# Fetching the tokens of two expert units at once, from two rounded parts of the normalised input

## The chip, the cores and the metric

The kernel runs on one core of one Trainium2 chip. The metric is the time of one execution on the device in microseconds; a kernel's time is the median of its runs. Engines are named as in the profile: PE is TensorE (matmuls), PEld its weight loads, DVE VectorE, ACT ScalarE, POOL GpSimd, and SP the engine whose queue issues the transfers that matter here.

## What is computed

The reference is a network of two blocks with two layers each, on 256 tokens of width 1024, all in fp32. The part that counts is the mixture of experts at the end of each layer of the second block:

```
x = _layernorm(alpha * x + mix, ln1_g[l], ln1_b[l])
ffn = _hier_moe(x, ...)            # 4 groups x 8 experts, top group, then top 2 in it
x = _layernorm(alpha * x + ffn, ln2_g[l], ln2_b[l])

def expert_block(args):
    xe, e = args                   # tokens sent to expert e
    hid = jax.nn.silu(xe @ w_gate[e]) * (xe @ w_up[e])
    return hid @ w_down[e]         # FFN width 256
```

Each expert's weights are 1024x512 (gate and up) and 256x1024 (down): 3 MiB, 96 MiB for the 32 experts of a layer. The first block has the same structure with RMS norm and an FFN width of 512; its experts use the same function with `centred` false.

## The kernel before

`moe` computes one layer of experts. The 32 experts are cut into 11 units; in block 2 their form is `wwwnwnwnnnw`. A w unit has 2 experts with room for 64 tokens each, an n unit 4 experts with room for 32 each, so every unit fills 128 rows. The first three units have fixed experts (0 to 5); the other places are given to the experts by how many tokens they have, by `Ranks`: its last product (L737) and a cast (L739) give the sorted numbers kidx, which SP loads into registers (L766) to address the weights of units 3 to 10.

A unit goes through these steps. `select` (L865) builds P, a 128-token by 128-row matrix per token half: a row's entry is the token's scale r (`tok`, from the norm) where the place number `pos` meets, else 0. `fetch(k)` (L871 and L879, for unit 0 `fetch_all`, L871, L877 and L879) multiplies eight 128x128 pieces of x by P in fp32 and applies scale and shift, which gives xg, the tokens of the unit, transposed. L1003 multiplies them by the gate and up weights (tile A), L1006 and L1007 form hid, `second` (L920) multiplies by the down weights (tile B), splits the result into two rounded parts yh and yl (L922, L923), and `combine` (L933) adds them back to the tokens in PSUM. `back` (L942 to L950) makes the weighted transposed P for that. While the products of unit n run, the select and fetch steps of unit n+1 are placed between them: half of them before the second product of the previous unit is complete, half behind it.

The weights pass through a ring of 1 MiB slots: 13 of the base and `EXTRA` more (9 in both blocks). The transfers are issued by SP at L176, in the order A0 A1 B0 A2 B1, then those that need kidx: A3 B2 A4 B3 ... B10, and behind them the weights of the next mixer. A slot can be refilled when the last product that reads it has run. Ahead of the unit before the last (`turn`) stands an `If` (L780) for the case of experts with more than 64 tokens (`overfull`); the branch isn't taken with these inputs, but all engines pass it.

`Head.finish` ends the layer norm ahead of the experts. Per token half it takes mean and variance, r by Ln and Exp (L608, L612), the logits (L621), subtracts the mean from x in place (L619) and a second Exp makes 1/r in `tok`. The residual of the layer multiplies x by r times alpha (L1932 and `residual_2`), and the routing weights are multiplied by 1/r (rwp, L906), because P holds r.

A type F32R (fp32r in the profile) appears in the mixers' products: x and weights are each split into a rounded high part and a low part (L397, L398), and products of the parts are summed.

Of the kernel before, what the change touches and what calls it, by code (L numbers as in the profile page):

```python
# [51 lines left out]
class Core:  # L52
# [25 lines left out]
    def constants(self, ctx):  # L78
# [30 lines left out]
        self.L = cp.tile([128, 2, 36], F32, name="logits")  # L109
        self.tok = cp.tile([128, 2, 4], F32, name="tok")  # L110
        self.gain = cp.tile([128, 8], F32, name="gain")
# [428 lines left out]
class Head:  # L540
# [58 lines left out]
    def finish(self, t):  # L599
        c, nc, p = self.c, self.c.nc, self.p  # L600
        r = c.tok[:, t, 0:1]
        l = p.tile([128, 2], F32, name=f"hl{t}")
        base = self.base[:, 0:36]
        if self.centred:
            mv = p.tile([128, 2], F32, name=f"hmv{t}")
            nc.vector.bn_aggr(mv, self.st[:, t])
            nc.vector.tensor_scalar(c.tok[:, t, 1:2], mv[:, 0:1], -1.0, None, op0=ALU.mult)
            nc.scalar.activation(l[:, 0:1], mv[:, 1:2], AF.Ln, bias=c.col(self.eps))  # L608
        else:
            nc.vector.tensor_scalar(l[:, 1:2], self.st[:, t, 0:1], 1.0 / D, self.eps, op0=ALU.mult, op1=ALU.add)  # L610
            nc.scalar.activation(l[:, 0:1], self.st[:, t, 1:2], AF.Ln, scale=1.0 / D, bias=l[:, 1:2])
        nc.scalar.activation(r, l[:, 0:1], AF.Exp, scale=-0.5)  # L612
        if self.centred:
            nm = p.tile([128, 1], F32, name=f"hnm{t}")
            nc.vector.tensor_scalar(nm, mv[:, 0:1], r, -1.0, op0=ALU.mult, op1=ALU.mult)
            base = p.tile([128, 36], F32, name=f"hb{t}")
            nc.vector.scalar_tensor_tensor(base, self.base[:, 36:72], nm, self.base[:, 0:36], op0=ALU.mult, op1=ALU.add)

            nc.scalar.activation(c.x[:, t], c.x[:, t], AF.Identity, bias=c.tok[:, t, 1:2])  # L619
        nc.scalar.activation(c.tok[:, t, 2:3], l[:, 0:1], AF.Exp, scale=0.5)  # L620
        nc.vector.scalar_tensor_tensor(c.L[:, t], self.q[:, 64 * t:64 * t + 36], r, base, op0=ALU.mult, op1=ALU.add)  # L621
        c.routed = self.end
# [202 lines left out]
def moe(c, ctx, index, scale, shift, w13, w2, nf, spare, centred, residual, end):  # L825
# [22 lines left out]
    extra = c.more(ctx, EXTRA[centred], "ring2", *XO[index])  # L848
    c.warm(sp.tile([128, 512], F32, name="s1")[:, :128], 9, c.routed)
    pos, as_, rest, chosen, counted = router(c, p, mp, c.L)  # L850
    c.warm(sp.tile([128, 512], F32, name="s2")[:, :128], 4, counted)
    places = {"pos": pos}

    def group(unit, first):

        e0, n, cap = unit
        P = p.tile([128, 2, 128], F32, name="P", bufs=2)
        P4 = P.rearrange("p t (g s) -> p t g s", s=cap)
        xg = p.tile([128, 8, 128], F32, name="xg", tag="xg", bufs=2)

        def select():
            at = pos if e0 < fixed else places["pos"]
            for t in range(2):
                for i in range(n):
                    selected = nc.vector.tensor_scalar(P4[:, t, i], c.iota[:, :cap], at[:, t, e0 + i:e0 + i + 1],  # L865
                                                       c.tok[:, t, 0:1], op0=ALU.is_equal, op1=ALU.mult)
            return selected

        def products(q, k, start):
            for t in range(2):  # L870
                nc.tensor.matmul(q, x[:, t, k * 128:(k + 1) * 128], P[:, t], start=start and t == 0, stop=t == 1,  # L871
                                 skip_group_check=True)

        def modulate(q, k, vector):
            o = xg[:, k]
            if vector:
# [4 lines left out]
        def fetch(k):  # L881
            def f():
                q = mp.tile([128, 512], F32, name="ms")[:, :128]
                products(q, k, True)
# [11 lines left out]
    P, xg, steps = group(units[0], True)  # L896
# [41 lines left out]
    def back(pr):  # L938

        e0, ne, cap = pr["unit"]  # L940
        Pw = p.tile([128, 2, 128], F32, name="Pw", bufs=2)
        nc.vector.tensor_mul(Pw.rearrange("p t (g s) -> p t g s", s=cap), P,  # L942
                             (wp if e0 < fixed else wk)[:, :, e0:e0 + ne, None].to_broadcast([128, 2, ne, cap]))
# [21 lines left out]
    for n, unit in enumerate(units):  # L965
        if n:
            P, xg = nxt[:2]
        nxt = group(units[n + 1], False) if n + 1 < len(units) else (None, None, [])
        e0, ne, cap = unit
        last = n == len(units) - 1  # L970
        todo = nxt[2]
        pr = {"n": n, "unit": unit, "h": []}
# [7 lines left out]
        if n == turn:  # L980
# [4 lines left out]
                                   skip_runtime_bounds_check_because="counts of tokens")  # L985
            overfull(c, sp, c.tok, scale, shift, out, w, pos, count, nf, *spare, gate, room,
                     hT, ranks)
# [7 lines left out]
        for u in range(steps_of):  # L995
            ws = begun if begun is not None and u == 0 else first(who, u)
            q = sp.tile([128, 512], F32, name="s1")
            for k in range(8):
                for i in range(128 // cap):

                    m, o = (i, 0) if centred else (i // 2, i % 2)
                    e = u * per + m
                    nc.tensor.matmul(q[cap * i:cap * i + cap, :], xg[:, k, e * cap:(e + 1) * cap],  # L1003
# [899 lines left out]

def residual_2(c, lnp, l, which, out, scale=None):

# [3 lines left out]
    for t in range(2):  # L1909
        nc.vector.scalar_tensor_tensor(out[:, t], c.x[:, t], ALPHA if scale is None else scale[:, t:t + 1], lnp[0],  # L1910
                                       op0=ALU.mult, op1=ALU.mult)
        nc.vector.scalar_tensor_tensor(out[:, t], lnp[1], ALPHA, out[:, t], op0=ALU.mult, op1=ALU.add)


def experts_2(c, l):

    nc, x = c.nc, c.x
    with ExitStack() as ctx:
# [10 lines left out]
        def residual(mp, keep, room, held):  # L1929
            out = keep.rearrange("p (t d) -> p t d", t=2)  # L1930
            sc = c.tok[:, :, 3]
            nc.vector.tensor_scalar(sc, c.tok[:, :, 0], ALPHA, None, op0=ALU.mult)  # L1932
            residual_2(c, [room[:, 0:1024], room[:, 1024:2048]], l, 0, out, sc)
            return out, None
# [324 lines left out]
```

## Time and profile before

| | |
|---|---|
| median of 3 runs | 2397.3 us (2396.76 to 2400.31) |
| the profiled execution | 2401.7 us, of which the span is 2399.7 |
| mean granted TensorE clock | 0.972 of full speed |
| TensorE (PE) busy | 2182.2 us, 91% of the span |
| VectorE (DVE), ScalarE (ACT) busy | 899.4 us, 774.6 us |
| moved by DMA | 775.20 MB, mean 323 GB/s |

The experts of block 2 lie at about 1640 to 1881 us (layer 0) and 2150 to 2386 us (layer 1) of the span. All times of rows are microseconds from the span's start. A window's row gives the busy time of each engine with the count of its instructions, then the granted clock, the DMA share and the rate. In rows of one group of instructions the first numbers are busy time and mean nanoseconds of one, then the idle time before them and what ended it.

### The profile page before, as it was taken

Reading aid. Unit: us, or ns where it says so; the run is one execution under the profiler, and the core shown is the slowest. Engines: PE = TensorE matmul, PEld = TensorE weight load, DVE = VectorE, ACT = ScalarE, POOL = GpSimd, SP = SyncE. Lnnn points to the kernel's source line nnn. Section 1 sums busy time; section 2 is a strip of 40 time slices with the busy share of each in tenths; the row PEclk is TensorE's granted clock in tenths of the full one; section 3 lists DMA queues with packets and bytes.
Section 4 is the critical chain, followed back from the end, with each engine's and each line's share of the span. In section 5 each row is a group of like instructions: output and inputs, shape, how many; then the busy total and the mean of one; then the engine's idle time right before and its main releaser. Section 6 shows DMA issues by size and latency. Waiting matters only on the chain. (4 is left out here: it accounts for less than half of the span.)

```text
span 2399.7 us, 33892 instructions
## 1 busy us (share of the span) xinstructions
PE 2182.2 (91%) x13034; PEld 1268.5 (53%) x13034; DVE 899.4 (37%) x2095; ACT 774.6 (32%) x1561; POOL 44.7 (2%) x48
## 2 busy tenths in 40 slices
PE   7999899988778989998877899999999899999997
PEld 4667633323225865333222387995444678984443
DVE  3864511111003753111100264984222547961232
ACT  3642311111113452211111254562222435642222
POOL 0001000000000200000000000000000000000000
PEclk8999999999999999999999998999999989999999
DMA  9977489999999347999999971556999923559997
GB/s 392 412 266 318 176 369 421 421 422 421 382 422 419 121 184 286 421 421 421 421 420 384 421 284 55 177 193 240 407 417 371 398 88 128 194 176 371 417 387 280
DMA packets 119852, 775.20 MB, mean 323 GB/s; under 512 B 14186, under 2 KB 15594, under 8 KB 35451
## 3 DMA queue, kind: packets, MB, share of 16 engines
q1 hardware_dynamic: 119674, 772.85, 80.1%
q8 instruction: 109, 1.79, 0.3%
q14 instruction: 69, 0.56, 0.1%
HBM read 771.75 MB, written 1.05 MB: 322 GB/s over the span
## 5 line engine op out<-in xcount | busy, mean ns | idle before, releaser
L1003 PE MATMUL s<-w,xg 128*32 128x512 f32 (+1 forms) x3072 | 577.2, 610 | 43.8 <-DMA w<-A 40.9
L920 PE MATMUL s<-w,ht 128*32 128x512 f32 (+1 forms) x1536 | 340.1, 612 | 37.9 <-DMA w<-B 36.4
L1003 PEld LDWEIGHTS s<-w,xg 128*32 128x32 f32 (+1 forms) x3072 | 131.6, 120 | 307.3 <-issue 199.0
L402 PE MATMUL pj<-hi,wh 128*128 128x256 f32 x864 | 242.8, 284 | 3.4 <-ACT sg L1785 2.3
L403 PE MATMUL pj<-lo,wh 128*128 128x256 f32 x864 | 243.2, 283 | 0.0
L871 PEld LDWEIGHTS ms<-P,x 128*128 128x128 f32 x1280 | 170.0, 195 | 138.5 <-ACT xg L879 75.0
L404 PE MATMUL pj<-hi,wl 128*128 128x256 f32 x864 | 240.1, 283 | 0.0
L923 DVE SCALAR_TENSOR_TENSOR yl<-s,ws,yh 128x512 fp32r<-128x512 f32 x88 | 66.1, 751 | 383.5 <-ACT yh L922 383.5
L871 PE MATMUL ms<-P,x 128*128 128x128 f32 x1280 | 208.2, 294 | 1.2
L920 PEld LDWEIGHTS s<-w,ht 128*32 128x32 f32 (+1 forms) x1536 | 80.1, 121 | 224.3 <-issue 147.3
L397 ACT ACTIVATE wh<-w 128x512 fp32r<-128x512 f32 x248 | 154.3, 630 | 119.4 <-PE pj L403 88.3
L398 DVE TENSOR_TENSOR wl<-w,wh 128x512 fp32r<-128x512 f32 x248 | 167.0, 688 | 49.4 <-ACT wh L397 45.1
L402 PEld LDWEIGHTS pj<-hi,wh 128*128 128x128 f32 x864 | 165.7, 192 | 9.1 <-ACT sg L1785 2.8
L404 PEld LDWEIGHTS pj<-hi,wl 128*128 128x128 f32 x864 | 164.0, 192 | 4.9 <-issue 2.4
L403 PEld LDWEIGHTS pj<-lo,wh 128*128 128x128 f32 x864 | 165.8, 192 | 0.5 <-issue 0.3
L865 DVE TENSOR_SCALAR P<-iota,kpos,tok 128x32 f32<-128x32 f32 (+1 forms) x216 | 49.4, 300 | 305.0 <-PE ms L871 304.9
L922 ACT ACTIVATE yh<-s,ws 128x512 fp32r<-128x512 f32 x88 | 60.5, 687 | 315.6 <-PE s L920 280.2
L1007 DVE TENSOR_TENSOR hid<-hid,s 128x256 f32<-128x256 f32 x66 | 27.7, 419 | 338.2 <-ACT hid L1006 338.1
L1006 ACT ACTIVATE hid<-s 128x256 f32<-128x256 f32 x66 | 25.3, 383 | 383.5 <-PE s L1003 383.2
L365 DVE TENSOR_TENSOR wl<-w,wh 128x512 fp32r<-128x512 f32 (+2 forms) x164 | 111.3, 689 | 100.6 <-ACT wh L364 86.0
L364 ACT ACTIVATE wh<-w 128x512 fp32r<-128x512 f32 (+2 forms) x164 | 99.5, 615 | 115.0 <-PE pj L350 55.9
L879 ACT ACTIVATE xg<-ms,mod,gain 128x128 f32<-128x128 f32 x160 | 72.8, 457 | 148.9 <-PE ms L871 146.0
(624 smaller groups left out, 2719.8 us busy)
## 6 DMA issues: line engine op xcount, KB each, us to landing
w<-A SPq DMA_DIRECT2D x384, 1024.0 KB, 19.1
w<-B SPq DMA_DIRECT2D x128, 1024.0 KB, 19.7
w<-B SPq DMA_DIRECT2D x128, 512.0 KB, 11.9
w<-ada SPq DMA_DIRECT2D x48, 1024.0 KB, 10.7
w<-wi SPq DMA_DIRECT2D x48, 1024.0 KB, 8.0
w<-w SPq DMA_DIRECT2D x26, 1024.0 KB, 16.7
w<-wo SPq DMA_DIRECT2D x16, 1024.0 KB, 7.3
w<-wbr SPq DMA_DIRECT2D x8, 1024.0 KB, 4.8
```

What stands on the lines that cost most here:

```text
L364: nc.scalar.activation(wh[:, :n], w[:, k], AF.Copy)
L365: nc.vector.tensor_sub(wl[:, :n], w[:, k], wh[:, :n].bitcast(F32))
L397: nc.scalar.activation(wh, w[:, k], AF.Copy)
L398: nc.vector.tensor_sub(wl, w[:, k], wh.bitcast(F32))
L402: nc.tensor.matmul(d, wh[:, e], hi, start=k == 0 and ch % 2 == 0, stop=False, skip_group_check=True)
L403: nc.tensor.matmul(d, wh[:, e], lo, start=False, stop=False, skip_group_check=True)
L404: nc.tensor.matmul(d, wl[:, e], hi, start=False, stop=k == nk - 1, skip_group_check=True)
L871: nc.tensor.matmul(q, x[:, t, k * 128:(k + 1) * 128], P[:, t], start=start and t == 0, stop=t == 1, skip_group_check=True)
L879: nc.scalar.activation(o, q, AF.Identity, bias=shift[:, k:k + 1], scale=scale[:, k:k + 1])
L920: nc.tensor.matmul(q[cap * i:cap * i + cap, :], ht[:, o * cap:o * cap + cap], pr["w2"][i][:, half, f * 512:f * 512 + 512], start=f == 0, s ...
L923: nc.vector.scalar_tensor_tensor(pr["yl"][:, half], q, pr["ws"], pr["yh"][:, half].bitcast(F32), op0=ALU.mult, op1=ALU.subtract)
L1003: nc.tensor.matmul(q[cap * i:cap * i + cap, :], xg[:, k, e * cap:(e + 1) * cap], ws[m][:, k, 512 * o:512 * o + 512], start=k == 0, stop=k ...
```

## The change

In block 2 the tokens are normalised before they are fetched: `Head.finish` scales x by r and adds -mean times r in one operation, so P holds only zeros and ones, the second Exp, the tok entry for the mean, the multiplication of the routing weights by 1/r and the scale of the residual go. x is kept in two fp32r parts: xh, a rounded copy (ScalarE), and xl = x - xh (`lower`, VectorE, four operations of 128x512). Units 1 to 10 are fetched in pairs, [1,2] to [9,10]: one P and one xg of twice the width for a pair, and per k and token half one product of xh and one of xl with 256 columns, in place of one fp32 product with 128 columns per unit. The eight steps of a pair are spread over its two units. `fetch_all` of unit 0 does all products with xh first, then those with xl. Select makes the ones of all experts of a unit and token half with one comparison of two broadcast tensors. `lower` is placed right behind the first select, ahead of fetch and `Ranks` in the text. The wider P and xg, xh and xl take 24 KB more of each partition: `EXTRA` becomes 9 and 6, so the ring of block 2 has 19 slots and not 22. Block 1 computes as before.

```diff
@@ Head.finish
-            nc.vector.tensor_scalar(c.tok[:, t, 1:2], mv[:, 0:1], -1.0, None, op0=ALU.mult)
...
-            nc.scalar.activation(c.x[:, t], c.x[:, t], AF.Identity, bias=c.tok[:, t, 1:2])
-        nc.scalar.activation(c.tok[:, t, 2:3], l[:, 0:1], AF.Exp, scale=0.5)
+            nc.scalar.activation(c.x[:, t], c.x[:, t], AF.Identity, scale=r, bias=nm)
+        else:
+            nc.scalar.activation(c.tok[:, t, 2:3], l[:, 0:1], AF.Exp, scale=0.5)
@@ moe
+    groups = [[0]] + [[n, n + 1] for n in range(1, len(units), 2)] if centred else [[n] for n in range(len(units))]
+    most = 128 * max(map(len, groups))
+    src = (x,)
+    if centred:
+        src = [p.tile([128, 2, 1024], F32R, name=n) for n in ("xh", "xl")]
+        for t in range(2):
+            nc.scalar.activation(src[0][:, t], x[:, t], AF.Copy)
     pos, as_, rest, chosen, counted = router(c, p, mp, c.L)
...
+    def lower(t):
+        for i in range(2):
+            d = slice(i * 512, i * 512 + 512)
+            nc.vector.tensor_sub(src[1][:, t, d], x[:, t, d], src[0][:, t, d].bitcast(F32))
...
+    def group(ns, first):
+
+        m = 128 * len(ns)
+        P = p.tile([128, 2, most], F32R if centred else F32, name="P", bufs=2)
+        P4 = [P[:, :, 128 * i:128 * i + 128].rearrange("p t (g s) -> p t g s", s=units[n][2]) for i, n in enumerate(ns)]
+        xg = p.tile([128, 8, most], F32, name="xg", tag="xg", bufs=2)
         def select():
-            at = pos if e0 < fixed else places["pos"]
+            for d, (e0, n, cap) in zip(P4, [units[n] for n in ns]):
+                at = pos if e0 < fixed else places["pos"]
+                for t in range(2):
+                    if centred:
+                        selected = nc.vector.tensor_tensor(d[:, t], c.iota[:, None, :cap].to_broadcast([128, n, cap]),
+                                                           at[:, t, e0:e0 + n, None].to_broadcast([128, n, cap]),
+                                                           ALU.is_equal)
...
+        def products(q, k, i, start):
             for t in range(2):
-                nc.tensor.matmul(q, x[:, t, k * 128:(k + 1) * 128], P[:, t], start=start and t == 0, stop=t == 1,
-                                 skip_group_check=True)
+                nc.tensor.matmul(q, src[i][:, t, k * 128:(k + 1) * 128], P[:, t, :m], start=start and t == 0,
+                                 stop=t == 1 and i == len(src) - 1, skip_group_check=True)
...
         def fetch_all():
             qs = [yp.tile([128, 512], F32, name="y", tag="y", bufs=4) for _ in range(4)]
-            for k in range(8):
-                q = qs[k % 4][:, (k // 4) * 128:(k // 4 + 1) * 128]
-                products(q, k, k < 4)
-                modulate(q, k, k % 2)
+            for i in range(len(src)):
+                for k in range(8):
+                    q = qs[k % 4][:, (k // 4) * m:(k // 4 + 1) * m]
+                    products(q, k, i, i == 0 and k < 4)
+                    if i == len(src) - 1:
+                        modulate(q, k, k % 2)
...
     selected = steps[0]()
+    if centred:
+        lower(0)
+        with tc.issue_after(selected.ins):
+            lower(1)
     for f in steps[1:]:
         f()
     with tc.issue_after(selected.ins):
         ranks = Ranks(c, p, mp, as_, fixed, wide, at)
         places["pos"] = ranks.ordered(pos, "kpos")
         w, cnt = rest(ranks.excess)
...
-    wp = p.tile([128, 2, 32], F32, name="rwp")
-    nc.vector.tensor_mul(wp, w, c.tok[:, :, 2:3].to_broadcast([128, 2, 32]))
+    wp = w
...
     for n, unit in enumerate(units):
-        if n:
-            P, xg = nxt[:2]
-        nxt = group(units[n + 1], False) if n + 1 < len(units) else (None, None, [])
+        g = next(i for i, ns in enumerate(groups) if n in ns)
+        at_unit = groups[g].index(n)
+        if at_unit == 0:
+            if n:
+                P, xg = nxt[:2]
+            nxt = group(groups[g + 1], False) if g + 1 < len(groups) else (None, None, [])
+            share = -(-len(nxt[2]) // len(groups[g]))
...
-        todo = nxt[2]
+        todo = [nxt[2].pop(0) for _ in range(min(share, len(nxt[2])))]
...
-EXTRA = (9, 9)
+EXTRA = (9, 6)
```

## Rows read from the trace of the kernel before

**Rows 1.** The page, parts 1 and 2: engines' busy time; rate in 40 slices.

```profile
PE 2182.2 (91%) x13034; PEld 1268.5 (53%) x13034; DVE 899.4 (37%) x2095; ACT 774.6 (32%) x1561; POOL 44.7 (2%) x48
...
GB/s 392 412 266 318 176 369 421 421 422 421 382 422 419 121 184 286 421 421 421 421 420 384 421 284 55 177 193 240 407 417 371 398 88 128 194 176 371 417 387 280
```

**Rows 2.** Windows: length, busy PE, PEld, DVE, ACT, POOL, clock, DMA share, GB/s.

```profile
1660.00:1820.00 160.00, 158.57 (x900) 68.09 (x899) 39.74 (x109) 44.67 (x95) 0.00 (x0) 0.99 1.01 414
1820.00:1840.00 20.00, 18.08 (x129) 8.70 (x128) 2.59 (x5) 5.11 (x11) 0.00 (x0) 1.00 0.75 283
...
2020.00:2060.00 40.00, 40.00 (x352) 40.00 (x351) 38.88 (x78) 22.33 (x41) 0.00 (x0) 1.00 0.59 206
2180.00:2320.00 140.00, 139.25 (x800) 60.25 (x802) 37.73 (x101) 41.21 (x86) 0.00 (x0) 1.00 1.02 416
2320.00:2340.00 20.00, 16.57 (x110) 7.90 (x106) 3.01 (x6) 5.52 (x12) 0.00 (x0) 0.98 0.79 324
2340.00:2360.00 20.00, 19.99 (x138) 9.01 (x130) 2.68 (x5) 5.50 (x12) 0.00 (x0) 0.94 0.98 364
```

**Rows 3.** Issues of tile w on SP, 1650 to 1900, and their landing.

```profile
L176 SPq DMA_DIRECT2D w<-B x56: 328/333/500, 1662.2 to 1862.6; - x56
...
L176 SPq DMA_DIRECT2D w<-A x52: 332/333/1101, 1656.6 to 1842.6; - x52
...
L176 SPq DMA_DIRECT2D w<-lnp x2: 338/338/339, 1765.3 to 1767.7; - x2
...
DMA to landing us min/median/max: 5.5/13.8/20.3
```

**Rows 4.** DMA view, the last B of layer 0: count, KB, us to landing.

```profile
w<-B SPq DMA_DIRECT2D x1, 512.0 KB, 10.2
```

**Rows 5.** Timeline of SP: first and last issues of layer 1's stream.

```profile
2164.53 1.19 SPq L176 DMA_DIRECT2D w<-A  x2
...
2366.70 4.06 SPq L176 DMA_DIRECT2D w<-B  x4
```

**Rows 6.** Waits of SP, 1655 to 1885: total us, times, longest.

```profile
SPq L176 <- PE s L1003: 25.6, 9, 10.6
SPq L766 <- DVE kidx L739: 19.5, 1, 19.5
SPq L780 <- SPq L780: 19.0, 1, 19.0
```

**Rows 7.** Timeline of DVE around the routing of layer 0: start, length.

```profile
1642.40 0.23 DVE L660 SCALAR_TENSOR_TENSOR rpos<-ms,ras 128x64 f32<-128x64 f32 x1 [0.72 <-PE ms L658]
1642.67 0.98 DVE L865 TENSOR_SCALAR P<-iota,rpos,tok 128x64 f32<-128x64 f32 x4
...
1648.99 0.22 DVE L735 TENSOR_SCALAR kperm<-krow,krank 32x32 f32<-32x32 f32 x1
...
1649.38 0.76 DVE L942 TENSOR_TENSOR Pw<-P,rwp 128x256 f32<-128x256 f32 x2
...
1655.72 0.18 DVE L739 CAST kidx<-ms 1x32 int32<-1x32 f32 x1 [1.88 <-PE ms L737]
```

**Rows 8.** Timeline of PE around the routing of layer 0.

```profile
1643.98 3.09 PE L871 MATMUL y<-P,x 128*128 128x128 f32 x16
...
1655.47 0.21 PE L737 MATMUL ms<-kperm,places 32*1 32x32 f32 x2
```

**Rows 9.** Timeline of PE, the last product of either layer.

```profile
1874.22 3.65 PE L920 MATMUL s<-w,ht 128*64 128x512 f32 x16
...
2379.83 3.65 PE L920 MATMUL s<-w,ht 128*64 128x512 f32 x16
```

**Rows 10.** Groups by line and shape, 1660 to 1820: the fetch products.

```profile
L871 PE MATMUL ms<-P,x 128*128 128x128 f32 x256 | 42.4, 292 | 0.2
```

**Rows 11.** The page, part 5: a subtraction into an fp32r low part.

```profile
L398 DVE TENSOR_TENSOR wl<-w,wh 128x512 fp32r<-128x512 f32 x248 | 167.0, 688 | 49.4 <-ACT wh L397 45.1
```

**Rows 12.** Timeline of ACT ahead of the routing of layer 0.

```profile
1636.91 1.14 ACT L619 ACTIVATE x<-x,tok 128x1024 f32<-128x1024 f32 x1
```

More of the change, by code (lines that the diff above doesn't have):

```diff
@@ L109, in constants @@
         self.L = cp.tile([128, 2, 36], F32, name="logits")
-        self.tok = cp.tile([128, 2, 4], F32, name="tok")
+        self.tok = cp.tile([128, 2, 3], F32, name="tok")
         self.gain = cp.tile([128, 8], F32, name="gain")
@@ L852, in moe @@
     places = {"pos": pos}
[L854 to L859, printed above, removed]
-        def select():
-            at = pos if e0 < fixed else places["pos"]
-            for t in range(2):
[L864 to L870, printed above, removed]
-                nc.tensor.matmul(q, x[:, t, k * 128:(k + 1) * 128], P[:, t], start=start and t == 0, stop=t == 1,
-                                 skip_group_check=True)
+    def lower(t):
+        for i in range(2):
+            d = slice(i * 512, i * 512 + 512)
+            nc.vector.tensor_sub(src[1][:, t, d], x[:, t, d], src[0][:, t, d].bitcast(F32))
@@ new lines, in group @@
+    def group(ns, first):
[3 more added lines that the diff above has]
+        xg = p.tile([128, 8, most], F32, name="xg", tag="xg", bufs=2)
+        def select():
+            for d, (e0, n, cap) in zip(P4, [units[n] for n in ns]):
[5 more added lines that the diff above has]
+                                                           ALU.is_equal)
+                        continue
+                    for i in range(n):
+                        selected = nc.vector.tensor_scalar(d[:, t, i], c.iota[:, :cap], at[:, t, e0 + i:e0 + i + 1],
+                                                           c.tok[:, t, 0:1], op0=ALU.is_equal, op1=ALU.mult)
+            return selected
+        def products(q, k, i, start):
+            for t in range(2):
+                nc.tensor.matmul(q, src[i][:, t, k * 128:(k + 1) * 128], P[:, t, :m], start=start and t == 0,
+                                 stop=t == 1 and i == len(src) - 1, skip_group_check=True)
@@ L874, in modulate @@
         def modulate(q, k, vector):
-            o = xg[:, k]
+            o = xg[:, k, :m]
             if vector:
@@ L882, in f @@
             def f():
-                q = mp.tile([128, 512], F32, name="ms")[:, :128]
-                products(q, k, True)
+                q = mp.tile([128, 512], F32, name="ms")[:, :m]
+                for i in range(len(src)):
+                    products(q, k, i, i == 0)
                 modulate(q, k, False)
@@ L889, in fetch_all @@
             qs = [yp.tile([128, 512], F32, name="y", tag="y", bufs=4) for _ in range(4)]
-            for k in range(8):
-                q = qs[k % 4][:, (k // 4) * 128:(k // 4 + 1) * 128]
-                products(q, k, k < 4)
-                modulate(q, k, k % 2)
+            for i in range(len(src)):
+                for k in range(8):
[3 more added lines that the diff above has]
+                        modulate(q, k, k % 2)
         return P4, xg, [select] + ([fetch_all] if first else [fetch(k) for k in range(8)])
-    P, xg, steps = group(units[0], True)
+    P, xg, steps = group(groups[0], True)
     selected = steps[0]()
+    if centred:
+        lower(0)
+        with tc.issue_after(selected.ins):
+            lower(1)
     for f in steps[1:]:
@@ L903, in moe @@
         w, cnt = rest(ranks.excess)
-    wp = p.tile([128, 2, 32], F32, name="rwp")
-    nc.vector.tensor_mul(wp, w, c.tok[:, :, 2:3].to_broadcast([128, 2, 32]))
+    wp = w
+    if not centred:
+        wp = p.tile([128, 2, 32], F32, name="rwp")
+        nc.vector.tensor_mul(wp, w, c.tok[:, :, 2:3].to_broadcast([128, 2, 32]))
     wk = ranks.ordered(wp, "kw")
@@ L941, in back @@
         Pw = p.tile([128, 2, 128], F32, name="Pw", bufs=2)
-        nc.vector.tensor_mul(Pw.rearrange("p t (g s) -> p t g s", s=cap), P,
+        nc.vector.tensor_mul(Pw.rearrange("p t (g s) -> p t g s", s=cap), P[at_unit].bitcast(F32),
                              (wp if e0 < fixed else wk)[:, :, e0:e0 + ne, None].to_broadcast([128, 2, ne, cap]))
@@ L985, in moe @@
                                    skip_runtime_bounds_check_because="counts of tokens")
-            overfull(c, sp, c.tok, scale, shift, out, w, pos, count, nf, *spare, gate, room,
+            overfull(c, sp, None if centred else c.tok, scale, shift, out, w, pos, count, nf, *spare, gate, room,
                      hT, ranks)
@@ L1001, in moe @@
                     m, o = (i, 0) if centred else (i // 2, i % 2)
-                    e = u * per + m
+                    e = at_unit * 128 // cap + u * per + m
                     nc.tensor.matmul(q[cap * i:cap * i + cap, :], xg[:, k, e * cap:(e + 1) * cap],
@@ L1901, in experts_1, with residual_2 @@
             lambda e: expert(c.a["B1"][l], e), 512, (w1_of, w2_of), False, residual, end)
-def residual_2(c, lnp, l, which, out, scale=None):
+def residual_2(c, lnp, l, which, out):
     nc = c.nc
@@ L1909, in residual_2 @@
     for t in range(2):
-        nc.vector.scalar_tensor_tensor(out[:, t], c.x[:, t], ALPHA if scale is None else scale[:, t:t + 1], lnp[0],
-                                       op0=ALU.mult, op1=ALU.mult)
+        nc.vector.scalar_tensor_tensor(out[:, t], c.x[:, t], ALPHA, lnp[0], op0=ALU.mult, op1=ALU.mult)
         nc.vector.scalar_tensor_tensor(out[:, t], lnp[1], ALPHA, out[:, t], op0=ALU.mult, op1=ALU.add)
@@ L1930, in residual @@
             out = keep.rearrange("p (t d) -> p t d", t=2)
-            sc = c.tok[:, :, 3]
-            nc.vector.tensor_scalar(sc, c.tok[:, :, 0], ALPHA, None, op0=ALU.mult)
-            residual_2(c, [room[:, 0:1024], room[:, 1024:2048]], l, 0, out, sc)
+            residual_2(c, [room[:, 0:1024], room[:, 1024:2048]], l, 0, out)
             return out, None
```

## The prediction

> **What bounds the kernel now.** I read the page first. TensorE is busy for 91% of the span and the input stream tops out at 421 to 422 GB/s [rows 1]; both look full, so averages do not say which one sets the two stages that the change touches. The windows do. In 160 us of the first expert stage of block 2 TensorE is busy for 158.57 us and the DMA share is 1.01 at 414 GB/s, and the second layer's stage reads the same [rows 2]. The two are tied, and the question is which one would still take as long if the other became faster.
>
> The ring's queue answers that. After the sorted expert numbers are known it issues 52 transfers of 1 MiB (w<-A), 56 of half a MiB (w<-B) and two lnp rows of half a MiB [rows 3]: 81 MiB. At 421.6 GB/s one MiB takes 2.487 us, so the stream can't be shorter than 201.5 us. It takes, in layer 0, from the first issue at 1656.6 to the last at 1862.6 [rows 3] plus 10.2 us to land [rows 4]: 216.2 us. Layer 1: 2164.53 to the end of the last group of issues at 2370.76, less the issue's own 0.33 [rows 3, 5], plus about the same 10.2: 216.1 us. So 14.7 us per layer are not transfer. Of these about 3.0 are the first landing (5.5 us, the shortest in [rows 3], less 2.5). About 6.6 lie in 1820 to 1840, where the queue delivers 283 of 421 GB/s [rows 2]: the waits show SP at L780 (the `If` of the overfull path) for 19.0 us [rows 6]. What ends that wait is the landing of SP's own transfers, not TensorE. The rest, about 5 us, is spread out.
>
> The start of the stream hangs on routing: SP waits 19.5 us for kidx [rows 6]. The places rpos stand at 1642.40 and kidx is cast at 1655.72, right behind a TensorE product (L737) at 1655.47 [rows 7, 8] that stands in order behind fetch and first expert products. The end of the stage is the last B: in layer 0 it lands at 1872.8, and the sixteen matmuls that need it run 1874.22 to 1877.87 [rows 9], 5.1 us after the landing. In layer 1 they end at 2383.48, 3.0 us after a landing at about 2380.5.
>
> **The change part by part.**
>
> *Fetch, steps of two units.* Now 256 records of L871 take 42.4 us in 160 us, 0.166 each [rows 10]; 8 steps of 4 make 5.3 us a unit and 10.6 a pair. Afterwards a pair takes 8 steps of 4 fp32r matmuls of 256 columns. The mixer window has 352 matmuls in 40.00 us, nearly all of that shape [rows 2], so 0.114 each: 3.6 us a pair. Saved: 7.0 us a pair, five pairs, 35 us of TensorE a layer. What this is worth on the path is another question: the stream needs its 201.5 us whoever computes. I take nothing for it in the middle of the stage. The ACT modulation becomes half as many operations of twice the width, off the path.
>
> *Tail.* With TensorE ahead, the last product should follow the landing in layer 0 as it does in layer 1: 5.1 becomes 2.8, so -2.3; layer 1, 0. Bounds -2.8 and 0.
>
> *Start of the stream.* The 32 fp32 records of unit 0's fetch become 16 with xh and 16 with xl, in fp32r, at 128 columns. The trace has no such product: from 0.057 (half of 0.114) to 0.166 (no gain), 1.8 to 5.3 us for 32. Four subtractions for xl are new, on VectorE; the nearest row is 128x512 at 0.688 [rows 11], so 2.75 us. Two stand ahead of the routing's own operations if the order keeps the text's order, two may fall among them. Against this, L737 now waits 1655.47 - 1643.98 = 11.5 us behind the start of the fetch [rows 8], of which 5.3 are fetch records and the rest are expert products already in hand. If routing is issued by its dependences alone: kperm now stands 6.8 us behind rpos, 3.1 of them behind sixteen fetch records [rows 7, 8]; with about 1.5 of fp32r in their place, 2.75 of subtractions and 0.6 for L737 and the cast that is 8.5 us behind rpos, where kidx now starts 13.3 behind it: -5. If all subtractions and all xl products go first, and unit 0's expert products with them: +1.5 to +3. I take -2 a layer, -4 in all, as 2 to 3 us of fetch records vanish and nothing else in the chain needs xl.
>
> *Head and select.* One small VectorE operation, one Exp and the residual's scale leave the routing chain, some 0.1 to 0.5 us. Scaling x now waits for r; L619 (1.14 us [rows 12]) moves behind Exp, and two copies to xh of the same shape follow: 3 x 1.14 from about 1638.1 is 1641.5, ahead of the select at 1642.67 [rows 7]. Without that cover a copy costs 1.14 us. Select becomes four operations for a pair; 128x256 took 0.38 [rows 7], so at most 1.5 us beside 2 x 0.98 now: VectorE is idle then, nothing on the path. The multiply rwp (0.2 us) goes, off the path.
>
> *The ring, 22 slots to 19.* Three slots are 7.5 us of stream. The queue already waits for TensorE to free slots, 25.6 us in 9 waits, longest 10.6 [rows 6], and no transfer rate is lost by it [rows 2], as the median transfer lands 13.8 us after its issue [rows 3]: about 11 us of earlier ones are still queued. With 19 slots the longest wait would be 10.6 + 7.5 = 18.1, less what TensorE has saved by then (3.5 us a unit; two to three units: 7 to 10). That leaves 8 to 11, about what is absorbed now. I take 0; the bounds are 0 and +7.5 a layer.
>
> *Spread dips.* A TensorE ahead frees slots earlier: of the about 5 us a layer I take 0.25 each, -0.5; bounds 0 and -4 each.
>
> *Not moved.* No transfer is added, removed or reordered on SP or POOL; the `If` still drains SP's transfers, so its 6.6 us stay.
>
> **Sum.** -2.3 - 4 - 0.5 = -6.8 us. The profiled execution took 2401.7 us (span 2399.7), that becomes 2394.9; on the median 2397.3 it is 2390.5 us, 0.28% less. The measurement tells a difference from about 0.2%, 4.8 us, so this is just beyond it.
>
> **Rivals.**
> - *Nothing at the start.* L737 is as late as now since xl takes the place of the fp32 passes; only the tail gains: 2394.5, within the bound. For it: the widest bound of that term has both signs.
> - *All losses of the stream go.* TensorE was behind the dips and behind the `If`: 2 x (14.7 - 3.0) and the tail, 2397.3 - 25.7 = 2371.6. Against it: SP's wait at L780 ends with its own transfers. (TensorE's whole 70 us, 2327, can't be had: 81 MiB don't fit.)
> - *Slower: the ring starves.* Place: the queue's longest slot wait, the first long n unit behind the fixed ones (reuse of the slots of unit 3). It decides once TensorE is less than some 7 us ahead there. Price 7.5 us a layer in place of the spread dips: 2390.5 + 15 = 2405.5, or about 2400 to 2407 with some of the lead. For it: this wait is on TensorE and long already.
> - *Slower: routing is late.* The four subtractions and every xl product stand ahead of L737: +3 to +4 a layer in place of -2, 2390.5 + 12 = 2402.5.
> - *The clock.* In 2340 to 2360, behind the gap of the `If` where TensorE was busy for 16.57 of 20 us, the granted clock averaged 0.94, as against 0.99 and 1.00 elsewhere [rows 2]; so part of that stretch ran at 1.2 and not 2.4 GHz. If longer waits for transfers pull the clock down at the tails, 3.65 us of L920 [rows 9] and the products behind it take twice as long: about +5 a layer, 2400.5. The Trainium skill, "TensorE: Matmul & The Clock Gate", section "HAM oscillation — how this bites in real kernels", describes this case, products shorter than the wait for the next slice, each starting on a throttled clock. By that rule a faster fetch would be given back; the trace agrees in that one place (0.94). The waits that I expect are short, so this has a small chance.
>
> **How the numbers follow.** Forecast 0.48; nothing at the start 0.26; ring 0.12; late routing 0.06; clock 0.04; all losses 0.04. Faster: 0.48 + 0.04 = 0.52; same: 0.26 + 0.04 = 0.30; slower: 0.12 + 0.06 = 0.18. The forecast's own range is 2380 (start -5 each, tail -2.8, some 5 us of dips) to 2392.5. The range for 8 in 10 reaches from there through the neutral case and into the slower ones: 2380 to 2404.
>
> **What would show it.** Right: L871 at about 0.11 to 0.12 a record and a third of its sum; TensorE busy for about 130 of the same 160 us with waits for w<-A and w<-B; DMA share still 1.0 at 414 GB/s or more; stream still about 214 to 216 us; kidx 11 us behind rpos. Wrong: a DMA share under 0.97 in the middle and slot waits beyond 15 us (ring); kidx over 14 us behind rpos (routing); a granted clock under 0.9 at the tail (clock); the wait at L780 shorter and its window over 350 GB/s (the losses were TensorE's).

## Result and profile after

The change makes the kernel slower: a median of 2411.5 us (2408.1 to 2413.1, 5 runs) against 2398.2 us (2396.8 to 2400.3, 5 runs), a ratio of 1.0057 with an interval of 1.0045 to 1.0068. The profiled execution took 2413.0 us with a span of 2411.2, 11.5 more than the span before.

The page of the changed kernel, part 1: TensorE has only 11 us less to do than before [rows 1].

```profile
PE 2171.0 (90%) x12714; PEld 1246.4 (52%) x12714; DVE 883.3 (37%) x2011; ACT 749.6 (31%) x1481; POOL 44.7 (2%) x48
```

Where the 11.5 us lie is read from SP's timeline: the first issue that needs kidx and the last B of either layer (the rows' last columns are the count of issues; the last issue of the second row starts at 1869.45 and lands 10.3 us later, that of the fourth starts at 2382.02). The traces hold no landing of the last B of layer 1; the 10.2 us that layer 0 of the kernel before shows is taken for it, here and for every run below, so the numbers of layer 1 that end at a landing may be off by a microsecond.

```profile
1663.46 4.92 SPq L176 DMA_DIRECT2D w<-A  x7
...
1849.12 20.66 SPq L176 DMA_DIRECT2D w<-B  x12
...
2173.42 1.26 SPq L176 DMA_DIRECT2D w<-A  x2
...
2380.86 1.49 SPq L176 DMA_DIRECT2D w<-B  x2
```

And from TensorE's last products:

```profile
1878.84 3.65 PE L948 MATMUL s<-w,ht 128*64 128x512 f32 x16
...
2391.39 3.65 PE L948 MATMUL s<-w,ht 128*64 128x512 f32 x16
```

In layer 0 the stream begins at 1663.46, 21.2 us behind rpos where it was 14.2; it lasts 216.3 us (216.2 before), and the last product ends 2.7 us behind the last landing (5.1 before). In layer 1 it begins 18.0 behind rpos (14.0 before), lasts 218.8 (216.1) and ends with the same 2.8 us. The sum is 7.0 + 4.0 + 0.1 + 2.7 - 2.4 = 11.4 us: the later start is 11.0 of it, and the longer stream of layer 1 and the shorter tail of layer 0 cancel. SP's waits from 1640 to 1900 show the wait for kidx as 29.3 us where it was 19.5 [rows 6]; SP comes to it 3.0 us sooner, and kidx is there 6.8 us later. The wait at the `If` is the same:

```profile
SPq L766 <- DVE kidx L739: 29.3, 1, 29.3
...
SPq L780 <- SPq L780: 19.0, 1, 19.0
```

VectorE's timeline around the routing of layer 0, to be read beside [rows 7]: two subtractions stand in the middle of the router (1638.91), two behind the select, and kidx comes 20.3 us behind rpos in place of 13.3, though kperm is there after 9.0.

```profile
1638.91 1.29 DVE L865 TENSOR_TENSOR xl<-x,xh 128x512 fp32r<-128x512 f32 x2 [0.31 <-ACT xh L857]
...
1642.27 0.23 DVE L660 SCALAR_TENSOR_TENSOR rpos<-ms,ras 128x64 f32<-128x64 f32 x1 [0.72 <-PE ms L658]
...
1642.94 1.29 DVE L865 TENSOR_TENSOR xl<-x,xh 128x512 fp32r<-128x512 f32 x2
...
1651.28 0.23 DVE L735 TENSOR_SCALAR kperm<-krow,krank 32x32 f32<-32x32 f32 x1
...
1662.55 0.18 DVE L739 CAST kidx<-ms 1x32 int32<-1x32 f32 x1 [3.38 <-PE ms L737]
```

TensorE's timeline of the same stretch, beside [rows 8] (in square brackets: idle time and what ended it).

```profile
1641.60 0.43 PE L657 MATMUL ms<-ras,lt 128*128 128x64 f32 x2 [2.38 <-DVE ras L655]
...
1644.32 3.67 PE L890 MATMUL y<-P,xh 128*128 128x128 f32 x16
...
1653.59 1.98 PE L1035 MATMUL s<-w,xg 128*64 128x512 f32 x4
...
1658.64 3.68 PE L1035 MATMUL s<-w,xg 128*64 128x512 f32 x6
1662.25 0.26 PE L737 MATMUL ms<-kperm,places 32*1 32x32 f32 x2
```

It idles 2.38 us ahead of the places product L657, then fetches 16 products with xh in 3.67 us, 0.229 each, double the 0.114 that the prediction took from a warm stretch. L737 runs at 1662.25, behind unit 0's products, which take 1.98 us for one k step (four records). The windows say why; the column before the last two is the granted clock:

```profile
1640.00:1644.00 4.00, 2.40 (x12) 2.19 (x12) 3.11 (x15) 0.00 (x0) 0.00 (x0) 0.77 0.28 109
1644.00:1648.00 4.00, 4.00 (x22) 3.97 (x22) 3.86 (x27) 1.67 (x3) 0.00 (x0) 0.50 0.00 0
1648.00:1652.00 4.00, 4.00 (x20) 3.09 (x20) 1.75 (x8) 1.37 (x3) 0.00 (x0) 0.50 0.00 0
...
1660.00:1664.00 4.00, 4.00 (x14) 0.92 (x13) 0.59 (x2) 0.00 (x0) 0.00 (x0) 0.67 0.00 0
```

The same windows of the kernel before:

```profile
1640.00:1644.00 4.00, 2.34 (x18) 2.03 (x17) 3.07 (x23) 0.00 (x0) 0.00 (x0) 0.85 0.89 328
1644.00:1648.00 4.00, 4.00 (x27) 3.85 (x27) 3.14 (x21) 2.58 (x5) 0.00 (x0) 0.73 0.02 7
1648.00:1652.00 4.00, 4.00 (x19) 1.67 (x17) 2.32 (x11) 0.46 (x1) 0.00 (x0) 1.00 0.00 0
```

Both kernels fall to 1.2 GHz as the router ends (in windows of 1 us the kernel before stands at 0.50 from 1643 to 1646 too). Before, the clock is down from 1642.8 to 1646.2, 3.4 us, and as long in layer 1; after, TensorE is fully busy (4.00 of 4.00 us) at half clock until 1662.6, 20 us. In layer 1 it is 13.7 us, from 2154.1 to 2167.8. In the middle of the stage the window [rows 2] reads

```profile
1660.00:1820.00 160.00, 156.42 (x842) 63.42 (x839) 32.83 (x76) 38.29 (x73) 0.00 (x0) 0.98 0.98 399
1820.00:1840.00 20.00, 12.59 (x79) 3.55 (x78) 1.84 (x4) 0.69 (x1) 0.00 (x0) 0.83 0.82 335
```

156.42 us busy where the prediction said about 130; this window still holds the late start, and from 1669 to 1820 the DMA share is 1.01 at 412 GB/s. The fetch products of all five pairs (line L890 alone, with xh and with xl, 1669 to 1820: busy PE, PEld, clock, DMA share, GB/s)

```profile
1669.00:1820.00 151.00, 27.47 (x160) 22.61 (x160) 0.99 1.01 412
```

are 27.5 us, 5.5 a pair, where [rows 10] gave 10.6: half as many records, but 0.17 each and not 0.114. They stand in steps of four among other products.

### The profile page after: what moved, and what is told of

It reads as the page before. It is cut to its first block, busy times and chain, and to the rows that moved or that the text cites. A ratio compares the mean times of both kernels' runs of the same rounds, so it can differ in the third digit from the quotient of the medians.

```text
span 2411.2 us, 33092 instructions
## 1 busy us (share of the span) xinstructions
PE 2171.0 (90%) x12714; PEld 1246.4 (52%) x12714; DVE 883.3 (37%) x2011; ACT 749.6 (31%) x1481; POOL 44.7 (2%) x48
## 5 line engine op out<-in xcount | busy, mean ns | idle before, releaser
L1035 PE MATMUL s<-w,xg 128*32 128x512 f32 (+1 forms) x3072 | 586.1, 618 | 50.8 <-DMA w<-A 41.2
L948 PE MATMUL s<-w,ht 128*32 128x512 f32 (+1 forms) x1536 | 349.5, 612 | 47.3 <-DMA w<-B 43.4
L1035 PEld LDWEIGHTS s<-w,xg 128*32 128x32 f32 (+1 forms) x3072 | 139.6, 121 | 347.6 <-issue 232.4
L948 PEld LDWEIGHTS s<-w,ht 128*32 128x32 f32 (+1 forms) x1536 | 80.4, 121 | 241.2 <-issue 144.8
L890 PEld LDWEIGHTS ms<-P,x 128*128 128x128 f32 x640 | 85.1, 198 | 68.5 <-issue 39.3
L350 PE MATMUL pj<-wl,hi 128*128 128x512 f32 (+2 forms) x272 | 107.0, 395 | 0.0
L890 PE MATMUL ms<-P,x 128*128 128x128 f32 x640 | 104.8, 297 | 0.7
## 6 DMA issues: line engine op xcount, KB each, us to landing
w<-B SPq DMA_DIRECT2D x128, 512.0 KB, 10.2
w<-ada SPq DMA_DIRECT2D x48, 1024.0 KB, 10.6
```

The costliest lines, as they stand in the source:

```text
L350: nc.tensor.matmul(qs[t][:, :n], a, wl[:, :n], start=False, stop=False)
L890: nc.tensor.matmul(q, src[i][:, t, k * 128:(k + 1) * 128], P[:, t, :m], start=start and t == 0, stop=t == 1 and i == len(src) - 1, skip_gr ...
L948: nc.tensor.matmul(q[cap * i:cap * i + cap, :], ht[:, o * cap:o * cap + cap], pr["w2"][i][:, half, f * 512:f * 512 + 512], start=f == 0, s ...
```

## Experiments

After the result there were these theories. *Clock:* routing is late because TensorE runs at 1.2 GHz, for a longer gap in the router (*gap*) or because the fp32r products of 128 columns keep the clock down (*shape*). *Order:* routing is late at any clock, since 32 fetch products and unit 0's expert products stand ahead of L737. *Ring:* the three slots cost the time. A table of all runs first; kidx is counted from rpos, the stream from its first issue to the landing of its last B, both of the profiled execution, in layers 0 and 1. Each ratio is taken against the kernel before in the same set of runs (its medians: 2398.2 us for the changed kernel, 2397.1 for e1 to e4, 2397.7 for e5 to e8, 2397.8 for e9 to e11).

| run | median us | ratio to before, 95% | kidx behind rpos | stream |
|---|---|---|---|---|
| before | 2397.3 | | 13.3, 13.2 | 216.2, 216.1 |
| changed | 2411.5 | 1.0057 (1.0045 to 1.0068) | 20.3, 17.1 | 216.3, 218.8 |
| e1 | 2411.7 | 1.0068 (1.0054 to 1.0082) | 13.3, 13.3 | 221.2, 220.6 |
| e2 | 2396.2 | 1.0000 (0.9991 to 1.0009) | 12.9, 13.8 | 215.0, 214.0 |
| e3 | 2397.0 | 1.0002 (0.9993 to 1.0011) | 11.4, 11.4 | 214.8, 215.7 |
| e4 | 2394.0 | 0.9985 (0.9976 to 0.9994) | 10.6, 11.8 | 215.6, 218.4 |
| e5 | 2394.7 | 0.9990 (0.9981 to 1.0000) | 11.6, 11.2 | 216.0, 216.3 |
| e6 | 2408.2 | 1.0043 (1.0026 to 1.0059) | 17.5, 16.7 | 217.6, 216.7 |
| e7 | 2397.7 | 0.9996 (0.9986 to 1.0006) | 6.3, 6.2 | 222.6, 223.2 |
| e8 | 2394.5 | 0.9993 (0.9983 to 1.0002) | 7.3, 7.4 | 218.8, 218.4 |
| e9 | 2397.9 | 1.0003 (0.9994 to 1.0012) | 13.3, 13.2 | 215.9, 215.2 |
| e10 | 2406.1 | 1.0040 (1.0027 to 1.0054) | 10.6, 11.8 | 220.7, 222.0 |
| e11 | 2394.4 | 0.9988 (0.9979 to 0.9997) | 10.6, 11.8 | 215.2, 216.3 |

Counting from rpos hides what the subtractions in the router delay, as rpos itself is later by it. From the start of the last logits product (L592) to kidx it is 18.8 and 18.6 us before, 26.5 and 23.7 after, 17.7 and 18.5 in e2, 17.7 and 17.7 in e3, 15.3 and 16.5 in e4.

**e1: three slots less, alone.**

```diff
-EXTRA = (9, 9)
+EXTRA = (9, 6)
```

> The kernel before, with the ring of block 2 at 19 slots and nothing else of the change. If the three slots are the cause of the 13 us (ring theory): about 7 us a layer, 2409 to 2413 us, and longer slot waits of SP with the DMA share under 1.0 in the middle of the stage. If the late routing is the cause (clock or order theory): the first issue behind kidx stays 14.2 us behind rpos in both layers and the stream loses at most some 3 us a layer, 2398 to 2404 us.

The ring theory's number came, 2411.7 us, and I had not believed in it. SP's waits of layer 0 (1640 to 1875), beside the 25.6 us of [rows 6], and a window beside the 414 GB/s of [rows 2]:

```profile
SPq L176 <- PE s L1003: 42.8, 8, 10.6
```

```profile
1680.00:1820.00 140.00, 139.16 (x813) 60.24 (x813) 35.07 (x90) 40.73 (x86) 0.00 (x0) 1.00 0.99 397
```

With the old fetch the slots are worth 14.6 us. That the changed kernel is as slow is a coincidence of sizes: its kidx is late and its stream is 0.1 and 2.7 us longer than before, here kidx is on time and the stream is 5.0 and 4.5 us longer.

**e2: the first two subtractions out of the router.**

```diff
     if centred:
-        lower(0)
         with tc.issue_after(selected.ins):
+            lower(0)
             lower(1)
```

> The changed kernel, with the first two subtractions of xl placed behind the first select as the other two are, so none stands between the router's operations. If the longer gap of TensorE ahead of the places (2.4 and over 2 us in place of 1.7) is what keeps the clock down (gap theory): the stretch at 1.2 GHz shrinks from 20 and 13 us to the 3 to 4 us of before, kidx comes 12 to 14 us behind rpos, 2396 to 2401 us. If the products of 128 columns in fp32r keep it down (shape theory): the stretch stays over 10 us, kidx 16 us or more behind rpos, 2407 to 2414 us. If the order alone makes routing late (32 fetch products ahead of L737): the clock may rise, yet 2407 us or more.

This one move takes the whole loss back: 2396.2 us, as before. TensorE's timeline and the windows:

```profile
1641.03 0.43 PE L657 MATMUL ms<-ras,lt 128*128 128x64 f32 x2 [0.91 <-DVE ras L655]
...
1642.78 2.00 PE L890 MATMUL y<-P,xh 128*128 128x128 f32 x16
1644.62 1.06 PE L890 MATMUL y<-P,xl 128*128 128x128 f32 x8
...
1654.34 0.21 PE L737 MATMUL ms<-kperm,places 32*1 32x32 f32 x2
```

```profile
1640.00:1644.00 4.00, 3.09 (x29) 2.84 (x28) 3.14 (x13) 0.73 (x1) 0.00 (x0) 1.00 0.53 213
1644.00:1648.00 4.00, 3.78 (x29) 2.67 (x28) 3.86 (x25) 2.59 (x6) 0.00 (x0) 1.00 0.00 0
```

The gap is 0.91 us, the clock does not fall before kidx is cast, and the same sixteen products take 2.00 us. As it did not fall, gap and shape are not yet apart. Behind kidx, at 1659.9, it does fall for 3.4 us, after a gap of 1.09 us ahead of L751. The kernel before has such a second fall too (at 1663.3, after a gap of 0.50); e4 has the same 1.09 us in both layers and falls in layer 1 alone. So the length of the last gap does not by itself tell whether the clock falls.

**e3: ten more warm-up products in the gap.**

```diff
-    c.warm(sp.tile([128, 512], F32, name="s1")[:, :128], 9, c.routed)
+    c.warm(sp.tile([128, 512], F32, name="s1")[:, :128], 19 if centred else 9, c.routed)
```

> The changed kernel, with ten more warm-up products ahead of the router in block 2 (19 in place of 9), which fill TensorE's gap; their result is used by nothing. Clock theories, gap or shape: if the clock never falls, the fetch of unit 0 runs at 0.115 us a product and kidx comes 11 to 13 us behind rpos; 2395 to 2401 us. Shape theory, if the shape alone can pull the clock down: it falls some us into the fetch and the time stays above 2405 us. Order theory: full clock, yet 2407 us or more. Should the warm-up hold up the place product L657, rpos is late by what it is too long.

The subtractions stay where the change has them, all 32 fetch products still stand ahead of L737, and only the gap is filled. The clock and VectorE's timeline:

```profile
1644.00:1648.00 4.00, 3.96 (x35) 3.59 (x36) 4.00 (x30) 2.72 (x6) 0.00 (x0) 1.00 0.00 0
1648.00:1652.00 4.00, 4.00 (x20) 1.36 (x18) 1.39 (x7) 0.68 (x2) 0.00 (x0) 1.00 0.02 4
```

```profile
1642.29 0.23 DVE L660 SCALAR_TENSOR_TENSOR rpos<-ms,ras 128x64 f32<-128x64 f32 x1 [0.72 <-PE ms L658]
...
1653.72 0.18 DVE L739 CAST kidx<-ms 1x32 int32<-1x32 f32 x1 [4.33 <-PE ms L737]
```

kidx is 11.4 us behind rpos, 8.9 less than in the changed kernel and 1.9 less than before. The order theory has fallen as the cause of the loss: at full clock the 32 products make kidx no later than before. Order still sets how long a low clock counts, as L737 waits behind unit 0's products in all these kernels (kperm is there at 1651.28 in the changed one, L737 runs at 1662.25).

**e4: unit 0 fetched in fp32, subtractions behind kidx** (`ranks.done` is the cast of kidx).

```diff
         def fetch_all():
...
-                    products(q, k, i, i == 0 and k < 4)
+                for t in range(2):
+                    nc.tensor.matmul(q, x[:, t, k * 128:(k + 1) * 128], P[:, t, :m].bitcast(F32),
+                                     start=k < 4 and t == 0, stop=t == 1, skip_group_check=True)
...
-        lower(0)
-        with tc.issue_after(selected.ins):
-            lower(1)
...
+        with tc.issue_after(ranks.done.ins):
+            lower(0)
+            lower(1)
```

> The changed kernel, with unit 0 fetched from the normalised x in fp32 as before (16 products of 4 passes), and the four subtractions of xl behind the cast of kidx. Both the added products and the subtractions are gone from the routing, so gap, shape and order theory alike expect kidx about 13 us behind rpos; the tail of layer 0 keeps its 2.3 us: 2395 to 2400 us. Ring theory: the three slots are still gone, 2405 us or more.

2394.0 us, 0.15% under the kernel before and a microsecond under what was expected; it is the lowest median, with e5, e8 and e11 within a microsecond of it. TensorE's timeline (the second row holds eight products, two records each):

```profile
1638.94 0.43 PE L657 MATMUL ms<-ras,lt 128*128 128x64 f32 x2 [0.90 <-DVE ras L655]
...
1640.69 2.05 PE L913 MATMUL y<-P,x 128*128 128x128 f32 x16
```

**e5 and e6: the gap put back, with either fetch.** The kernels of e4 (e5) and e2 (e6) with 2 warm-up products.

```diff
-    c.warm(sp.tile([128, 512], F32, name="s1")[:, :128], 9, c.routed)
+    c.warm(sp.tile([128, 512], F32, name="s1")[:, :128], 2 if centred else 9, c.routed)
```

> The kernel of e4 (unit 0 fetched in fp32, subtractions behind kidx), with 2 warm-up products ahead of the router in place of 9, so that TensorE idles some 2.6 us ahead of the places, as long as in the changed kernel. If the length of the gap alone decides how long the clock stays down: 13 to 20 us at 1.2 GHz, kidx 16 us or more behind rpos, 2405 to 2412 us. If the fp32r products of 128 columns keep it down: the fp32 fetch lets it rise after some 4 us as in the kernel before, kidx 12 to 14 us behind rpos, 2395 to 2400 us.

> The kernel of e2 (fetch of unit 0 in fp32r parts, subtractions behind the select), with the same 2 warm-up products: the gap is back without any subtraction in the router. Both clock theories: the clock falls and stays down for 13 us or more, kidx 16 us or more behind rpos, 2405 to 2414 us. If the subtractions and not the gap were what e2 removed: as e2, 2394 to 2399 us.

The gaps ahead of L657 are alike, 2.47 us in e5

```profile
1642.83 0.69 PE L657 MATMUL ms<-ras,lt 128*128 128x64 f32 x2 [2.47 <-DVE ras L655]
```

and 2.46 us in e6:

```profile
1642.15 0.69 PE L657 MATMUL ms<-ras,lt 128*128 128x64 f32 x2 [2.46 <-DVE ras L655]
```

The clock of e5 behind them,

```profile
1644.00:1648.00 4.00, 4.00 (x21) 3.76 (x21) 3.83 (x28) 1.67 (x3) 0.00 (x0) 0.50 0.02 4
1648.00:1652.00 4.00, 4.00 (x29) 2.80 (x29) 2.26 (x10) 1.36 (x3) 0.00 (x0) 0.97 0.00 0
```

and of e6:

```profile
1644.00:1648.00 4.00, 4.00 (x23) 3.76 (x21) 4.00 (x20) 0.80 (x3) 0.00 (x0) 0.50 0.01 4
1648.00:1652.00 4.00, 4.00 (x21) 3.79 (x20) 3.33 (x17) 1.76 (x3) 0.00 (x0) 0.50 0.00 0
1652.00:1656.00 4.00, 4.00 (x13) 1.60 (x14) 0.87 (x4) 0.92 (x2) 0.00 (x0) 0.50 0.00 0
1656.00:1660.00 4.00, 4.00 (x16) 1.17 (x12) 0.41 (x1) 0.00 (x0) 0.00 (x0) 0.77 0.00 0
```

After the same gap, the clock is back at 1648.2 when the work behind it is the fp32 fetch, and at 1657.8 when it is the fp32r fetch: 5.4 and 15.7 us behind L657, and in layer 1 4.5 and 14.2. Both are needed for the loss: the gap makes the clock fall, and it stays down in the version with the new fetch. Both fetches have 128 columns, so the width does not tell them apart. But e5 and e6 differ in one thing more than the form of the products, the place of the four subtractions; in e6 the last of them ends at 1646.4, 11 us before the clock is back, and no run has the fp32r fetch without them. That the fp32r form alone keeps the clock down is therefore likely, not shown. It fits that in layer 0 of e6 and of the changed kernel the clock comes back during or right behind the first longer run of unit 0's fp32 products, eight records from 1655.01 and six from 1658.64, with no fp32r product among them. e6 has no subtraction in the router, so what those in the changed kernel did was to make the gap.

**e7 and e8: unit 0's expert products behind L737,** in e4 (with the subtractions behind the copy of kpos) and in the kernel before.

```diff
-            for k in range(8):
+            with tc.issue_after(ranks.sorted.ins) if centred and n == 0 else nullcontext():
+                for k in range(8):
...
```

> The kernel of e4, with unit 0's expert products ordered behind L737 on TensorE and the subtractions behind the copy of kpos. If the start of the stream sets the end of the layer: kidx 7 to 8 us behind rpos (10.6 and 11.8 in e4), 3 to 4 us less a layer, 2385 to 2389 us. If the ring of 19 slots or TensorE takes it back in the first units: 2391 to 2395 us.

> The kernel before, with unit 0's expert products ordered behind L737 and nothing else. If the start of the stream sets the end: kidx 8 to 9 us behind rpos in place of 13.3, 4 to 5 us less a layer, 2387 to 2390 us. If TensorE sets the stage with the old fetch: the expert products are only moved, and 2395 to 2399 us stays.

Both start the stream 4 to 6 us sooner, and little or nothing of it arrives: e7 lies above both of its ranges, e8 between the two. In e7, SP's waits up to 1700 and two windows:

```profile
SPq L176 <- PE s L1036: 21.8, 6, 6.3
...
SPq L176 <- PE s L948: 8.1, 3, 6.7
```

```profile
1670.00:1690.00 20.00, 19.71 (x92) 8.50 (x91) 3.73 (x10) 4.97 (x9) 0.00 (x0) 1.00 0.88 320
1690.00:1710.00 20.00, 20.00 (x120) 8.27 (x122) 3.14 (x7) 5.92 (x11) 0.00 (x0) 1.00 0.96 359
```

The stream is 7 and 5 us longer than in e4: it begins before the first slots are free again, waits for them, and delivers 320 and 359 GB/s. With 22 slots (e8) it is 2.4 us longer a layer; the ratio's interval just includes no change.

**e9: less TensorE work at 22 slots.** The kernel before; the fetch of units 1 to 10 leaves out the second half of the tokens.

```diff
-                products(q, k, True)
+                nc.tensor.matmul(q, x[:, 0, k * 128:(k + 1) * 128], P[:, 0], start=True, stop=True,
+                                 skip_group_check=True)
```

> The kernel before with 22 slots, where the fetch of units 1 to 10 leaves out the second half of the tokens (one fp32 product per k in place of two), so that TensorE saves some 26 us a layer and nothing else changes; the output lacks those tokens' shares. If the prediction's step is right that TensorE's saving is worth only the tail and small dips at 22 slots: 2 to 5 us in all, 2392 to 2396 us, with the stream still 214 to 216 us. If TensorE paces the stream through the slots: 10 us or more, under 2388 us, and a stream under 210 us.

Window and fetch group, beside [rows 2, 10]:

```profile
1660.00:1820.00 160.00, 152.75 (x813) 58.40 (x812) 42.55 (x114) 47.45 (x105) 0.00 (x0) 0.99 1.02 417
```

```profile
L884 PE MATMUL ms<-P,x 128*128 128x128 f32 x144 | 29.9, 306 | 0.9 <-ACT xg L879 0.8
```

A unit's 16 records take 3.3 us where 32 took 5.3; from 1640 to 1880 the fetch is busy for 32.9 us and not 51.5, so 19 us a layer are gone (not 26, as records in twos take 0.21). The time is the same, just above the range expected if the saving is worth only the tail and small dips. The stream is as long as before, and the lag of layer 0 falls only from 5.1 to 4.5 us: with less to do TensorE waits more, and from 1840 to 1860 the clock stands at 0.89 where it was 1.00. At 22 slots less fetch work in the middle is worth nothing that can be measured.

**e10: two more slots taken from e4.** `EXTRA = (9, 4)`.

> The kernel of e4 with two slots fewer again, 17. If with the faster fetch the ring of 19 slots is only just long enough: a slot costs about its 2.5 us, 4 to 5 us a layer, 2401 to 2405 us. If the new fetch leaves room: 2393 to 2397 us. e1 showed 7 us a layer for three slots with the old fetch.

2406.1 us, 12.1 over e4 and a little over the range for a ring that is only just long enough. The new fetch has no room to spare below 19 slots: SP's waits for TensorE from 1640 to 1700 grow from 26.7 us in e4 to 32.6, and the stream by 5.1 and 3.5 us. (The profiled execution took 2400.1 us, 6 less than the median, so the trace shows only a part.)

**e11: e4 with the subtractions behind kperm,** where VectorE waits for L737.

> The kernel of e4 with the four subtractions behind kperm, in the time in which VectorE waits for L737, and no longer ahead of the copy kT. If they fit there: kidx as in e4 or up to 1 us later, TensorE no longer waits 1.1 us for kT, no stretch at 1.2 GHz in the first units, 2391 to 2395 us. If they hold up kidx: 1 to 2.5 us later a layer, 2395 to 2398 us.

2394.4 us, as e4. They fit there, as kidx stands where it did, and gain nothing that can be told; the wait for kT that was to go is still 1.09 us.

## Why the prediction was wrong

**The step that failed** is the term of the start of the stream, "I take -2 a layer". It measured +7.0 and +4.0 us, and the whole 2411.5 us where 2390.5 was forecast. What I left out was the clock in that place. I had the clock as a rival, but put it at the tail behind the `If`, and priced it at 5 us a layer with a chance of 0.04; I never looked at the granted clock of the routing of the kernel before, whose window 1644 to 1648 stands at 0.73. There it had fallen already, and any edit that made the gap longer or changed what runs behind it was at risk. The subtractions were counted as VectorE's 2.75 us on the chain and as nothing for TensorE, which waits for that chain with nothing to do.

The gain in that term is not shown either. It set about 1.5 us of fp32r against 3.1 us for sixteen fp32 records, but those 3.1 us were read where the clock was down; at full clock the same records take 2.05 us (e4) and sixteen fp32r products with xh 2.00 (e2). In e3 kidx is 1.9 and 1.7 us sooner behind rpos than before (1.1 and 1.0 counted from L592). That is about what 3.4 us at half clock cost the kernel before, by estimate 1.7 us.

**The rival "routing is late"** named the place and the sign, at +3 to +4 a layer, but for a reason that e3 refutes (order, at full clock). **The rival "the clock"** named the mechanism in another place. Its sign came too, 0.83 from 1820 to 1840, but cost nothing that shows there: the lag behind the last landing is 2.7 and 2.8 us.

**The ring, taken at 0 with bounds 0 and +7.5 a layer.** The upper bound is what the slots cost alone: e1, 14.6 us on both layers. That the rest of the change buys it back is shown by e1 and e2, both with 19 slots: 2411.7 and 2396.2, with streams of 221.2 and 220.6 us against 215.0 and 214.0. So 0 was about the right net, and a close one (e10). That it is the lead of the faster fetch that does it is argued: SP's waits for L1003 and L920 of 47.5 us in e1 are 34.5 in e2 (L1035 and L948, 1640 to 1875), but no run has the old kernel's other parts with the new fetch at 19 slots. The sign that was to show this rival, a slot wait beyond 15 us, would have missed it: the longest in e1 is 10.6. The fetch's saving on TensorE was over-sized: 5.1 us a pair where I had 7.0.

**Nothing in the middle.** Right: e9, and in layer 0 a stream of 216.3 us after as before; in layer 1 it is 2.7 us longer, which stays open. **`If`.** Right: 19.0 us of waiting at L780 in both.

**Tail.** The size was right: the lag of layer 0 fell from 5.1 to 2.7 us, that of layer 1 stayed. The reading that the last sixteen products wait for the last B was not. In both kernels they run behind other products without a gap, and the last wait for a transfer in layer 0 of the changed kernel is for the last A:

```profile
1864.36 3.65 PE L1035 MATMUL s<-w,xg 128*64 128x512 f32 x14 [0.92 <-DMA w<-A]
```

From there to the end of the last product it is 18.1 us of products and of waits for ScalarE and VectorE. Layer 1 ends in the same way in both kernels, 18.2 and 18.1 us behind the landing of the last A.

**The sum without the clock.** -6.8 was forecast. The profiled span of e3 is 7.3 less than that of before, but its median is 0.1 us less (interval of the ratio 0.9993 to 1.0011). The profiled execution of before, on which my terms rest, was itself 4.4 us over its median, that of e3 2.9 us under its own; so part of what I read as losses (5 us of spread dips and the long lag of layer 0) may have been that execution's own. How much of the rest lies in the start, which e7 and e8 show to be worth less than its length, and how much in the slots, the runs don't tell apart.

**The Trainium skill**, "TensorE: Matmul & The Clock Gate", section "HAM oscillation — how this bites in real kernels", describes products that are shorter than the wait for their next data, each of which starts on a throttled clock. The trace agrees in part: in the router the clock falls with gaps of 1.7 to 2.5 us and stays up where the gap is 0.9 (e2, e4), though 2.25 us of warm-up products stand ahead of the 1.7 us in the kernel before. Waits alone don't explain this case: in the changed kernel the clock stayed at 1.2 GHz through 20 us in which TensorE had no gap.

## What to carry to other kernels

Read the granted clock in windows of a few microseconds at every place where TensorE waits for a chain of small operations, before moving work into that chain: 1.3 us of VectorE's work in such a chain cost about 14 us here. A stream through a ring is bound by its slots and by the engine that frees them together; taking slots and speeding that engine up can cancel, so try each alone. And a gain of a fraction of a per cent should be worked out against several executions, not one whose time is not the median.

## What the runs showed of the hardware

An fp32r product of 128 columns took 0.115 us at 2.4 GHz (in e2 sixteen fill the 1.84 us from 1642.78 to 1644.62), as much as one of 256 columns (0.114, [rows 2]): half the columns saved nothing, so two rounded parts at 128 columns (0.23) are hardly faster than one fp32 product (8 in 2.05 us, 0.25, e4). After the same idle gap of TensorE the clock came back some 10 us later behind an fp32r fetch than behind an fp32 one (e5, e6, both layers), with TensorE fully busy in both. In the changed kernel and in e6, in both layers, it came back during or right behind the first longer run of unit 0's fp32 records (six to eight) with no fp32r product among them. Why the chip treats them differently is not shown by these runs.
